# A two-layer decoder step: factors of q and k moved into v and the norm's epsilon, three more jobs ahead of the retention, third sums in banks of their own

## The chip, the cores and the metric

The kernel runs on one core of one Trainium2 chip. The metric is the device time of one execution in microseconds. The core's engines are TensorE (PE in the profile, its weight loads PEld), VectorE (DVE), ScalarE (ACT), GpSimd (POOL) and SyncE (SP), which here issues most of the transfers. Each runs its instructions in the order in which they were written out when the program was built, and waits on semaphores for the others.

## The reference, cut to what matters

The model is one inference step for 512 prompt tokens and 32 sample tokens (8 sequences of 4), 544 columns in all. Layer 0 is a gated short convolution, layer 1 a multi-scale retention with 4 heads of 256 key and 512 value channels; a SwiGLU feed-forward stage follows each. The change concerns layer 1:

```python
z = x @ w_in                                   # x is rms-normalized
q, k, v, g = split(z)                          # 4 heads each
q = rotary(q, pos)
k = rotary(k, pos) * (HEAD_DK ** -0.5)
o, S = retention_chunkwise(q, k, v, s0)        # powers of gamma(h) by position
mu, var = mean(o), mean((o - mu) ** 2)         # over the 512 value channels
of = (o - mu) * rsqrt(var + GN_EPS) * gn_g
out = (silu(g) * of) @ w_out
```

Per token there are scalar factors on q, k and v: the reciprocal root mean square of the token (the norm's gain goes elsewhere) and a power of gamma that carries the decay. A factor that belongs to the query's token scales the whole row of `o` and so leaves the group norm unchanged but for the epsilon. A factor that belongs to the key's token can as well be put on the value of that token.

## The kernel before, in words

All products are in 32-bit, split into a high and a low part, with three matmuls for each (high by high, high by low, low by high). Activations lie as channel tiles of 128 partitions by 544 tokens; the tokens are worked on in two halves of 272 columns. A *plain projection* of one 128-channel output block is 8 channel tiles x 3 x 2 halves = 48 matmuls (`project`, line 175). A *job* (`Job`, `run`, `weights7`; matmuls at line 480) makes two output blocks at once with seven products of smaller blocks in the place of eight: 7 x 4 x 3 = 84 matmuls. It adds and subtracts weight blocks on VectorE (lines 438 to 441), splits the combinations (lines 190, 191, 423 to 425), holds a first sum, a second sum and a third sum in banks, and copies or adds the sums into an SBUF tile as they come (lines 540, 543, 844). The banks are of two kinds: `sm`, four single banks in rotation (`bank`), and `mm`, two pairs of banks (`psum`).

The stages, in order of time: the convolution; feed-forward stage 0 as jobs; a stretch *ahead* of the retention, inside feed-forward stage 0's pools; the retention; feed-forward stage 1; the last norm.

The stretch ahead makes q and k of head 0 by plain projections and stores them in memory unscaled (`qk_made`, line 806), makes R, the factors by token (line 263), and then runs five jobs for gates: two blocks of head 0 and all four blocks of heads 1 and 2. Finished gates are stored in memory (`gate_made`, line 851) and fetched again in their head.

In the retention each head does, in program order: `value` (v of the head, 96 wide matmuls at lines 999 to 1001; in the midst of it the splits of q and k, the sample scores at line 1194 with line 1198, the keys' transposes, and in heads 1 and 2 the split of the head before, `held_parts`), two `state` steps, `scores`, and four `inner` products for the four blocks of 128 tokens. Between them stand *fills*, pieces of independent work for TensorE: in head 0 two gate projections and the two k projections of head 1, in heads 1 and 2 the output projections of the head before (*held products*, eight of 24 matmuls), in head 3 its own four gate projections. Four state tiles per head are loaded (line 1210), used (line 1222), updated on VectorE (line 1243) and stored (line 1244). Each block's result is normalized (lines 1144 to 1148, a power on POOL at line 227), transposed (line 1172) and multiplied into the gates (lines 1178, 1182). q and k of the next head are projected in the tail of a head: from head 1 on k twice among the last steps and q twice after all of them. From each bank the projection is multiplied with a factor table (line 959, `gt`, loaded at line 915 and scaled by R at line 942), and after the second block both are rotated with six operations (lines 969 to 974). Head 3 ends with held products of head 2 and its own output projection.

The order on each engine is made by a scheduler when the program is built; program order is its priority, and `issue_after` keeps instructions behind a named one. Buffers are rotated by tag: a new tile waits for the last user of the oldest buffer of its tag. Two lines that the change turns on:

```python
w3, w1 = [wts.tile([P, 2 * n], F32, tag="w", name=nm("w")) for _ in range(2)]
self.c = bank()[:, :HT]
```

Of the kernel before, what the change touches and what calls it, by code (L numbers as in the profile page):

```python
# [49 lines left out]
def hybrid_decode_kernel(ctx: ExitStack, tc: tile.TileContext, a: dict, o: dict):  # L50
# [52 lines left out]
    nc.vector.memset(expo, -0.5)  # L103
# [26 lines left out]
    last_load = [None]  # L130
# [93 lines left out]
    def rsqrt(out, var, n):  # L224

        nc.vector.tensor_scalar_add(out, var, EPS)
        nc.gpsimd.tensor_tensor(out, out, expo[: out.shape[0], :n], op=ALU.pow)
# [199 lines left out]

    def weights7(src1, src2, sw, adding=False):
# [6 lines left out]
        last_load[0] = nc.sync.dma_start(w1, src1)  # L435
# [25 lines left out]
    class Job:  # L461
# [3 lines left out]
        def __init__(self, srcs, operand, sw, take):  # L465
            self.srcs, self.operand, self.sw, self.take = srcs, operand, sw, take
# [27 lines left out]
        def middle(self):  # L494
            for which in self.order:
# [3 lines left out]
                elif which == 5:  # L499
                    self.c = bank()[:, :HT]  # L500
# [48 lines left out]
    def ffn(layer, next_gain, then=None):  # L549
        with ExitStack() as c1:  # L550
# [4 lines left out]
            lp = c1.enter_context(tc.tile_pool(name=f"ffl{layer}", bufs=1, reuse_waits="tile"))  # L555

# [226 lines left out]
    gate_made = {h: dram.tile([P, 4, T], F32, tag=f"g{h}", name=nm("gm")) for h in (0, *AHEAD)}  # L783

    def ahead(tp, fp, sw, operand_tiles):

# [16 lines left out]
        for which, two in ((1, pts), (0, qs)):  # L803
            for dt, pt in enumerate(two):
                each(lambda p, d: nc.scalar.activation(d, p, AF.Copy), pt, halves(made[which][:, dt, :]))
            nc.scalar.dma_start(qk_made[which], made[which])

# [25 lines left out]
        def gates(h, n):  # L833
# [19 lines left out]
            return Job([a["rtg"][h, n + i] for i in range(2)], operand, sw, summed(tile2, gate))  # L853
# [8 lines left out]
    with ExitStack() as c2:  # L862
# [47 lines left out]
        def qk_start(h):  # L910

            st = {}
            gt = kp.tile([P, 2, T], F32, tag="gt", name=nm("gt"), bufs=1)
            with tc.issue_after(last_load[0].ins) if h == 0 else ExitStack():
                nc.sync.dma_start(gt, a["gtab"][h])
            st["gt"] = gt
            st["rot"] = [
                pool.tile([P, 2, T], F32, tag=f"rot{w}", name=nm("rot"), bufs=1) for w, pool in enumerate((tp, kp))
            ]
            return st  # L920

        def qk_loaded(st):

            for t, src in ((st["rot"][1], qk_made[1]), (st["rot"][0], qk_made[0])):
                with tc.issue_after(last_load[0].ins):
                    nc.sync.dma_start(t, src)
            for which in (1, 0):
                qk_scale(st, which)
                r = st["rot"][which]
                nc.vector.tensor_mul(r, r, st["gt"][:, which, :].unsqueeze(1).to_broadcast([P, 2, T]))  # L930
# [8 lines left out]

        def qk_scale(st, which):  # L940
            gi = halves(st["gt"][:, which, :])
            nc.vector.tensor_mul(gi, gi, R)

        def qk_project(h, st, which, dt, inside=None):
# [9 lines left out]
            qk_rotate(st, which, dt, pt)  # L954

        def qk_rotate(st, which, dt, pt):
            r = st["rot"][which]
            each(
                lambda p, ri, gi: nc.vector.tensor_mul(ri, p, gi), pt, halves(r[:, dt, :]), halves(st["gt"][:, which, :])
            )  # L960
            if dt:
                rotate(r, *products())
# [4 lines left out]
        def rotate(r, t0, t1, c=slice(0, T)):  # L967
# [4 lines left out]
            nc.vector.tensor_mul(r[:, 1, :], r[:, 1, :], cos[:, c])  # L972
            nc.vector.tensor_sub(r[:, 0, :], r[:, 0, :], t0)
# [9 lines left out]
        def swapped(second, shape, dtype, name):  # L983

            return (tp if second else vp).tile(shape, dtype, tag="gate" if second else "vyl", name=nm(name), bufs=1)

        def value(h, st):
# [4 lines left out]
            for c in range(4):  # L992
# [19 lines left out]
                if c == 1:  # L1012
                    qk_split(h, st, 1)
                    qk_split(h, st, 0)
                    sample_scores(h, st)
                    for dt in range(2):
                        qsrc = st["rot"][0][:, dt, SEQ:].rearrange("p (g r s) -> p g r s", g=4, r=2)
                        for r in range(2):
                            nc.vector.tensor_scalar_mul(
                                qm[:, dt, :, r, 4 * r : 4 * r + 4], qsrc[:, :, r, :], _gamma(h) ** 4  # L1020
# [481 lines left out]
```

## Time and profile before

| what | value |
|---|---|
| median of 3 runs | 1458.92 us (1457.52 to 1459.11) |
| the profiled execution's own time | 1461.27 us |
| its span | 1459.5 us |
| mean granted TensorE clock | 0.996 |
| TensorE / VectorE / ScalarE / GpSimd busy | 99% / 68% / 45% / 10% |
| moved by the DMA engines | 201.89 MB, 138 GB/s mean |

The profile is one execution. Its page gives busy times by engine, the chain of work that ended last (followed back from the last instruction, at each step to what released it), and groups of instructions by line, engine and tile. A wait is given as "engine line <- what it waited for: total us, times, longest". A row of the timeline is start, length, engine, line, operation, out<-in, shapes, count, with the idle time before it in brackets. A row of stretches gives the busy time of each engine with the number of its instructions, then the granted clock, the share of the DMA engines and GB/s. Times within the trace are from the start of the span. TensorE's matmuls overlap, so one lasts about 290 ns although a new one starts every 125.

### The profile page before, as it was taken

How to read it: one execution, taken by the hardware profiler on the slowest of the kernel's cores; microseconds unless marked ns; L12 is line 12 of the kernel's file. 1: busy time of each engine (PE TensorE's matmuls, PEld its weight loads, DVE VectorE, ACT ScalarE, POOL GpSimd, SP SyncE). 2: the span in 40 equal slices, each digit the busy share in tenths (PEclk: the TensorE clock that was granted, in tenths of full speed). 3: DMA queues.
4: the chain of work that ended last, by engine and by line, in shares of the span. 5: the costliest groups of instructions: out<-in, count | busy, mean ns of one | idle time of the engine just before them, and what ended most of it. 6: DMA issues, size and time to landing. Idle time of an engine off the chain costs nothing.

```text
span 1459.5 us, 26302 instructions
## 1 busy us (share of the span) xinstructions
PE 1443.8 (99%) x10860; PEld 1369.0 (94%) x10860; DVE 985.7 (68%) x1536; ACT 664.0 (45%) x971; POOL 147.9 (10%) x184
## 2 busy tenths in 40 slices
PE   9999999999999999999999999999999999999997
PEld 8999999999999999997878888878999999999997
DVE  5644679847748648677575765845699848749554
ACT  5222466626526437664223032134386626537334
POOL 0100011101101003210010000000111101101002
PEclk9999999999999999999999999999999999999998
DMA  6222246636536434767353734724666635546432
GB/s 219 82 88 92 86 114 140 150 116 126 143 106 139 124 80 133 195 167 262 125 191 116 258 106 144 274 92 143 175 138 149 153 108 131 131 109 148 119 81 77
DMA packets 84297, 201.89 MB, mean 138 GB/s; under 512 B 8129, under 2 KB 25409, under 8 KB 83921
## 3 DMA queue, kind: packets, MB, share of 16 engines
q1 hardware_dynamic: 67296, 165.91, 35.9%
q0 software_dynamic: 15008, 29.18, 12.2%
q10 hardware_dynamic: 1872, 5.12, 0.9%
q8 instruction: 85, 1.39, 0.4%
q14 instruction: 36, 0.29, 0.1%
HBM read 175.11 MB, written 25.08 MB: 137 GB/s over the span
## 4 chain that ended last, share of the span: by engine, by line
PE 89%; DVE 5%; DMA 3%; ACT 1%; issue 1%; POOL 0%; SPq 0%; DVEq 0%; ACTq 0%; POOLq 0%
PE sm L480 35%; PE mm L175 33%; PE sm L175 7%; PE sm L999 2%; PE sm L1000 2%; PE sm L1001 2%; PE sm L163 2%; PE sm L164 1%; PE sm L165 1%; PE sm L1222 1%; DMA w<-in_ffgu_dram 1%; DVE wl L191 1%; DMA w<-in_rtg_dram 1%; DVE S L1243 1%; DVE ol L191 1%
## 5 line engine op out<-in xcount | busy, mean ns | idle before, releaser
L190 ACT ACTIVATE wh<-w 128x1024 fp32r<-128x1024 f32 (+4 forms) x126 | 115.8, 923 | 318.8 <-PE mm L175 204.9
L480 PE MATMUL sm<-oh,wh 128*128 128x272 f32 x744 | 215.5, 290 | 0.1
L480 PE MATMUL sm<-ol,wh 128*128 128x272 f32 x744 | 214.3, 288 | 0.7 <-DVE ol L191 0.7
L480 PE MATMUL sm<-oh,wl 128*128 128x272 f32 x744 | 213.9, 287 | 0.0
L175 PE MATMUL mm<-xh,wh 128*128 128x272 f32 x844 | 176.3, 290 | 1.1 <-ACT wh L190 1.0
L175 PE MATMUL mm<-xh,wl 128*128 128x272 f32 x844 | 174.5, 289 | 0.4 <-DMA wl<-in_rtqk_dram 0.4
L175 PE MATMUL mm<-xl,wh 128*128 128x272 f32 x844 | 173.9, 287 | 0.0
L480 PE MATMUL sm<-oh,h 128*128 128x272 f32 x568 | 164.1, 289 | 0.5 <-DVE gate L543 0.4
L480 PE MATMUL sm<-oh,l 128*128 128x272 f32 x568 | 163.5, 288 | 0.0
L480 PE MATMUL sm<-ol,h 128*128 128x272 f32 x568 | 163.5, 288 | 0.0
L273 DVE TENSOR_TENSOR x<-x,mm 128x544 f32<-128x544 f32 x90 | 64.7, 719 | 144.7 <-PE mm L175 144.7
L191 DVE TENSOR_TENSOR wl<-w,wh 128x1024 fp32r<-128x1024 f32 (+4 forms) x126 | 134.2, 1071 | 23.7 <-ACT wh L190 22.3
L480 PEld LDWEIGHTS sm<-oh,wh 128*128 128x128 f32 x744 | 139.8, 188 | 2.1 <-ACT gate L540 0.9
L423 ACT ACTIVATE wh<-w 128x1024 fp32r<-128x1024 f32 x97 | 102.8, 1060 | 83.2 <-PE sm L480 56.1
L480 PEld LDWEIGHTS sm<-ol,wh 128*128 128x128 f32 x744 | 139.8, 188 | 0.9 <-DVE ol L191 0.9
L480 PEld LDWEIGHTS sm<-oh,wl 128*128 128x128 f32 x744 | 140.3, 189 | 0.0
L426 POOL DMA_DIRECT2D wl<-in_ffgu_dram x87 | 75.6, 869 | 635.2 <-ACT wl L425 261.5
L175 PEld LDWEIGHTS mm<-xh,wh 128*128 128x128 f32 x844 | 132.2, 188 | 5.4 <-ACT wh L190 1.4
L175 PEld LDWEIGHTS mm<-xh,wl 128*128 128x128 f32 x844 | 131.6, 188 | 0.9 <-DMA wl<-in_rtqk_dram 0.6
L175 PEld LDWEIGHTS mm<-xl,wh 128*128 128x128 f32 x844 | 132.1, 188 | 0.1
L191 DVE TENSOR_TENSOR l<-w,h 128x1024 fp32r<-128x1024 f32 x98 | 93.4, 955 | 27.0 <-ACT h L190 26.4
L480 PEld LDWEIGHTS sm<-oh,h 128*128 128x128 f32 x568 | 107.2, 189 | 1.0 <-ACT wh L423 0.6
(296 smaller groups left out, 3211.8 us busy)
## 6 DMA issues: line engine op xcount, KB each, us to landing
w<-in_ffgu_dram SPq DMA_DIRECT2D x88, 512.0 KB, 3.9
wl<-in_ffgu_dram POOLq DMA_DIRECT2D x87, 256.0 KB, 4.8
w<-in_ffdn_dram SPq DMA_DIRECT2D x96, 192.0 KB, 2.5
S<-in_rets_dram SPq DMA_DIRECT2D x16, 1024.0 KB, 7.0
out_rets_dram<-S SPq DMA_DIRECT2D x16, 1024.0 KB, 4.8
w<-in_cvin_dram SPq DMA_DIRECT2D x21, 512.0 KB, 3.4
w<-in_rtqk_dram SPq DMA_DIRECT2D x16, 512.0 KB, 3.6
w<-in_rtg_dram SPq DMA_DIRECT2D x16, 512.0 KB, 4.1
```

The source lines that it names most:

```text
L163: nc.tensor.matmul(out, lh, rh, start=start, stop=False, skip_group_check=True)
L164: nc.tensor.matmul(out, lh, rl, start=False, stop=False, skip_group_check=True)
L175: last_product[0] = nc.tensor.matmul(half(pt, hf)[:, :HT], w[:, c], act[k][:, hf * HT : (hf + 1) * HT], start=(first and k == ks[0] and i ...
L190: h = nc.scalar.activation(dh, src, AF.Copy)
L191: last_low[0] = nc.vector.tensor_sub(dl, src, dh.bitcast(F32))
L273: last_residual[0] = nc.vector.tensor_add(xk, xk, p)
L423: nc.scalar.activation(wh, w, AF.Copy)
L426: nc.gpsimd.dma_start(wl[:, n:], src[:, n:], accum_op=ALU.add)
L480: last = nc.tensor.matmul(out, w[:, c], b, start=(first and k == 0 and i == 0), stop=(k == KP - 1 and i == 2), skip_group_check=True,)
L999: nc.tensor.matmul(out, xh[kt][:, ts_], wh[:, cw], start=(kt == 0), stop=False)
L1000: nc.tensor.matmul(out, xh[kt][:, ts_], wl[:, cw], start=False, stop=False)
L1001: last = nc.tensor.matmul(out, xl[kt][:, ts_], wh[:, cw], start=False, stop=(kt == KT - 1))
```

## The change

Factors. q and k are no longer multiplied with a table by token. Two small tables are made once, during the jobs ahead (`factors`): `fv`, by which v is scaled (the power of gamma times the token's norm factor squared, one norm factor being that of k), and `fe`, the epsilon of the group norm for each prompt token, divided by the square of the factor left out of q. They come from eight small loads of the table, two transposes, two powers and a few small operations. For the 32 sample tokens the factor of q is put into the masked queries and the sample scores (`gs`, from a small load `fq`).

Rotation. Since nothing is to be multiplied first, q and k go from the bank directly into products with cosine and sine: two products per block, then one sum and one difference.

Jobs ahead. Eight in the place of five: (head, first block) = (0, 0), (1, 0), (1, 2), k of 2, (2, 0), (2, 2), k of 3, (3, 0). k of heads 2 and 3 is stored unrotated (`k_made`), fetched in the head before, and rotated there behind the second state update. Heads 1 and 2 then project only q of the next head; head 3 projects only its gates 2 and 3, has no third fill, and does held products 2 and 3 in its fourth.

Banks. In the jobs ahead the third sum takes an `mm` bank.

Weights. In every job the first source is loaded before the second; the fourth combination has a pool of its own with two buffers. The stored k of head 0 is loaded behind the first weight load of the last job, q behind the second.

```diff
-    def rsqrt(out, var, n):
+    def rsqrt(out, var, n, eps=None):
-        nc.vector.tensor_scalar_add(out, var, EPS)
+        if eps is None:
+            nc.vector.tensor_scalar_add(out, var, EPS)
+        else:
+            nc.vector.tensor_add(out, var, eps)
...
     def weights7(src1, src2, sw, adding=False):
-        w3, w1 = [wts.tile([P, 2 * n], F32, tag="w", name=nm("w")) for _ in range(2)]
+        w1, w3 = [wts.tile([P, 2 * n], F32, tag="w", name=nm("w")) for _ in range(2)]
-        w4 = sw.tile([P, n], F32, tag="w4", name=nm("w4"))
+        w4 = fourth[0].tile([P, n], F32, tag="w4", name=nm("w4"))
+        second_load[0] = nc.sync.dma_start(w1, src1)
         last_load[0] = nc.sync.dma_start(w3, src2)
-        last_load[0] = nc.sync.dma_start(w1, src1)
...
-                    self.c = bank()[:, :HT]
+                    self.c = self.third()[:, :HT]
...
+        ft = tp.tile([P, 3, P], F32, tag="gu", name=nm("ft"))
+        for t in range(4):
+            nc.sync.dma_start(ft[t * NH : (t + 1) * NH, 0, :], a["gtab"][:, 0, 1, t * P : (t + 1) * P])
+        for t in range(4):
+            nc.sync.dma_start(ft[:NH, 1, t * NS : (t + 1) * NS], a["gtab"][:, 0, 1, SEQ:])
+        def factors():
+            pt = bank()
+            nc.tensor.transpose(pt[:, : 4 * NH], ft[: 4 * NH, 0, :], ident[: 4 * NH, : 4 * NH])
+            nc.tensor.transpose(pt[:, 4 * NH : 5 * NH], ft[:NH, 1, :], ident[:NH, :NH])
+            tab = pt[:, : 4 * NH].rearrange("p (t h) -> p t h", h=NH)
+            ri = ft[:, 2, :4]
+            nc.gpsimd.tensor_tensor(ri, rN[:, :4], expo[:, 6:7].to_broadcast([P, 4]), op=ALU.pow)
+            scale, back = [r.unsqueeze(2).to_broadcast([P, 4, NH]) for r in (rN[:, :4], ri)]
+            nc.vector.tensor_mul(fv[:, :4, :], tab, scale)
...
+            nc.vector.tensor_mul(fe, tab, back)
+            nc.vector.scalar_tensor_tensor(fe, fe, 256.0 * EPS, fe, op0=ALU.mult, op1=ALU.mult)
+            nc.vector.tensor_mul(fv[:, :4, :], fv[:, :4, :], scale)
...
-        jobs = [gates(0, 0)] + [gates(h, n) for h in AHEAD for n in (0, 2)]
+        jobs = [gates(*hn) for hn in ((0, 0), (1, 0), (1, 2), (2, None), (2, 0), (2, 2), (3, None), (3, 0))]
         jobs[0].prepare()
-        run(jobs, (2, 5, 6), lambda i: None, iter(()))
+        run(jobs, (2, 5, 6), lambda i: factors() if i == 1 else None, iter(()))
...
             r = st["rot"][which]
-            each(lambda p, ri, gi: nc.vector.tensor_mul(ri, p, gi), pt, halves(r[:, dt, :]), halves(st["gt"][:, which, :]))
+            if dt == 0:
+                st["rt"] = products()
+            for d, by in ((st["rt"][1 - dt], sin), (r[:, dt, :], cos)):
+                each(lambda p, d, f: nc.vector.tensor_mul(d, p, f), pt, halves(d), halves(by))
             if dt:
-                rotate(r, *products())
+                turned(r, *st["rt"])
...
             nc.vector.tensor_mul(ss, pt[:NS, 0, :NS], mask_s[:NS])
+            nc.vector.tensor_mul(ss, ss, st["gs"][:NS])
...
                 if h in AHEAD:
                     for i in range(2):
                         held_project(h, (0, 4, 2, 6)[n] + i)
-                elif h:
-                    gate_project(h, st, n)
                 elif n < 2:
                     gate_project(h, st, n + 2)
-                else:
+                elif more:
                     qk_project(h + 1, nxt, 1, n - 2)
+                elif n == 3:
+                    held_parts(h, older)
+                    held_project(h, 2)
+                    held_project(h, 3)
...
             if h in AHEAD:
                 st["gate"] = [swapped(h == 2, [P, 4, T], F32, "gate")]
                 nc.sync.dma_start(st["gate"][0], gate_made[h])
+                if more:
+                    nxt = qk_places(h + 1)
+                    nc.sync.dma_start(nxt["rot"][1], k_made[h + 1])
...
             states_update(h, st, 1)
+            if more and h:
+                with tc.issue_after(last_update[0].ins):
+                    rotate(nxt["rot"][1], *products())
...
-                    qk_project(h + 1, nxt, int(h > 0), 0)
+                    qk_project(h + 1, nxt, 0, 0)
...
             gated_pair(h, st, (yns, 4), (yn3, 3))
-            if more and h:
-                qk_project(h + 1, nxt, 0, 0)
-                qk_project(h + 1, nxt, 0, 1)
```

More of the change, by code (lines that the diff above doesn't have):

```diff
@@ L461, in hybrid_decode_kernel, with __init__ @@
     class Job:
-        def __init__(self, srcs, operand, sw, take):
-            self.srcs, self.operand, self.sw, self.take = srcs, operand, sw, take
+        def __init__(self, srcs, operand, sw, take, third=None):
+            self.srcs, self.operand, self.sw, self.take, self.third = srcs, operand, sw, take, third or bank
         order = (6, 5, 2)
@@ L555, in ffn @@
             lp = c1.enter_context(tc.tile_pool(name=f"ffl{layer}", bufs=1, reuse_waits="tile"))
+            fourth[0] = c1.enter_context(tc.tile_pool(name=f"ffw{layer}", bufs=2, reuse_waits="tile"))
             def operand_tiles(i, blocks):
@@ L1102, in gate_project @@
         def gate_project(h, st, n):
-            st.setdefault("gate", [])
-            if h == NH - 1 and n % 2 == 0:
-                pool, tag = ((kp, "gt"), (qp, "qkhl1"))[n // 2]
-                t = pool.tile([P, 2, T], F32, tag=tag, name=nm("gate"), bufs=1)
-                st["gate"].append(t)
-            elif not st["gate"]:
-                st["gate"].append(swapped(True, [P, 4, T], F32, "gate"))
+            if n == 2:
+                last = h == NH - 1
+                t = kp.tile([P, 2, T], F32, tag="gt", name=nm("gate"), bufs=1) if last else swapped(True, [P, 4, T], F32, "gate")
+                st["gate"] = [None, t] if last else [t]
             wh, wl = load_piece(a["rtg"][h, n], KT * P)
```

110 lines of the change are left out of this document (57 added, 53 removed).

## The prediction, made before the result was known

> **What bounds the kernel now.** I read the page first, then the chain that ended last, TensorE's waits, and the stages that the change touches.
>
> ```profile
> span 1459.5 us, 26302 instructions
> PE 1443.8 (99%) x10860; PEld 1369.0 (94%) x10860; DVE 985.7 (68%) x1536; ACT 664.0 (45%) x971; POOL 147.9 (10%) x184
> ```
>
> TensorE is busy for 99% of the span, so the time is the price of its matmuls plus a few stalls. The chain gives the price of each kind of matmul (start, length, what):
>
> ```profile
> 427.63 63.12 PE sm L480 x504
> 634.88 18.09 PE sm L480 x128
> 756.93 0.99 PE mm L1007 x8
> 804.08 6.23 PE mm L175 x48
> 859.67 0.99 PE mm L1007 x8
> 885.67 6.01 PE mm L175 x48
> 1265.60 36.00 PE mm L175 x288
> ```
>
> The 504 matmuls of line 480 (six seven-product jobs) take 125.2 ns each and the 288 of line 175 (plain projections) 125.0 ns. A job of 84 matmuls does two weight blocks in 63.12/6 = 10.52 us; two plain projections of 48 take 2 x 6.01 = 12.02 us. TensorE's waits and the timeline show the one large stall, between two jobs ahead of the retention:
>
> ```profile
> PE sm L480 <- DVE gate L543: 2.2, 2, 1.8
> PE sm L480 <- DVE ol L191: 0.7, 1, 0.7
> ...
> PEld sm L480 <- DVE gate L543: 2.0, 1, 2.0
> ...
> 631.24 1.36 DVE L942 TENSOR_TENSOR gt<-gt,R 128x544 f32<-128x544 f32 x2 [0.29 <-DMA gt<-in_gtab_dram]
> 633.19 1.29 DVE L930 TENSOR_TENSOR rot<-rot,gt 128x1088 f32<-128x1088 f32 x1 [0.59 <-DMA rot<-qkm]
> 634.40 0.43 DVE L543 TENSOR_TENSOR gate<-gate,sm 128x272 f32<-128x272 f32 x1
> 634.88 0.39 PE L480 MATMUL sm<-xh,h 128*128 128x272 f32 x1 [1.80 <-DVE gate L543]
> ```
>
> VectorE stands in line behind the factor table and the stored k (two transfers that it waits for), so the addition of line 543 that empties a bank comes late, and the next job's product finds no free bank: all four `sm` banks rotate through first, second and third sums alike. The stall costs more than its own length:
>
> ```profile
> 628.00:632.50 4.50, 4.50 (x35) 4.15 (x34) 3.03 (x5) 1.72 (x5) 0.87 (x1) 1.00 1.02 341
> 636.20:639.20 3.00, 3.00 (x15) 3.00 (x15) 2.75 (x6) 1.15 (x2) 0.00 (x0) 0.50 0.71 102
> 640.00:644.00 4.00, 4.00 (x34) 4.00 (x33) 3.70 (x8) 3.42 (x6) 0.53 (x1) 1.00 0.51 145
> ```
>
> In these stretches (TensorE's busy time and matmuls first, its granted clock third from the right) the clock is 1.00, then 0.50, then 1.00: 15 matmuls in 3.0 us (5.0 per us) against 34 in 4.0 us (8.5 per us). On 128 matmuls from 634.88 the chain spent 18.09 us, where 128 x 125.2 ns are 16.0; some 0.7 us of that is the usual change between products, so I take 1.4 us for the slow clock.
>
> **The change part by part.**
>
> *Work on TensorE.* Heads 2 and 3 lose two plain k projections each, head 3 two gate projections: 6 x 48 = 288 matmuls, 36.0 us by the last row of the chain. Three jobs come ahead: 3 x 84 = 252 matmuls, 63.12/2 = 31.6 us. Net -4.4 us. This holds wherever they stand, because TensorE is the bound in both stages.
>
> *Banks.* The third sums get `mm` banks; the four `sm` banks serve first and second sums, so a bank is asked for again a full job (10.5 us) after its last use. The factor table is no longer loaded or scaled on VectorE, and the stored k is fetched after the first weight load of the last job, not after the second. Both causes of the stall go: -2.0 us (the weight load's wait; the matmul's is 1.8), and -1.4 us of slow clock. What is late next there is the store-and-rotate work of VectorE, covered by the 10 us for which the weights are prepared ahead. Ends: 0 (another wait takes its place) and -3.8.
>
> *Weights in the jobs.* The order of the two loads and a second buffer for the fourth combination let one weight tile go sooner. TensorE waits for none of it in 44 jobs of the feed-forward stages, so 0.
>
> *Factors.* Two transposes of 0.1 us and a bank for some microseconds; six VectorE operations on 20 columns or fewer (0.16 us by the like row below) and two powers on POOL. Eight small loads go through SP ahead of weight loads; each holds SP 0.33 us:
>
> ```profile
> 571.53 0.33 SPq L435 DMA_DIRECT2D w<-in_rtg_dram  x1
> 581.47 0.33 SPq L905 DMA_DIRECT2D sqacc<-in_rope_dram  x1
> ...
> 582.77 0.16 DVE L226 TENSOR_SCALAR rN<-sm 128x6 f32<-128x6 f32 x1
> 583.02 2.26 POOL L227 TENSOR_TENSOR rN<-rN,expo 128x6 f32<-128x6 f32 x1 [7.36 <-DVE rN L226]
> ```
>
> SP is idle for 9.6 us between those two loads, more than 8 x 0.33 = 2.6 us. The factor operation of VectorE that needs the power waits behind POOL, 2.3 us like the row at 583.02, once, with a job of cover: +0.3 us in all, ends +0.2 and +2.5.
>
> *Sample scores.* One more multiplication on a chain that TensorE waits on a little, and a new one for the sample factors before it (early, covered by the value projection):
>
> ```profile
> 758.08 0.18 DVE L1198 TENSOR_TENSOR ss<-mm,cb 32x32 f32<-32x32 f32 x1 [2.92 <-PE mm L1194]
> ...
> PEld mm L899 <- ACT s L190: 1.5, 4, 0.4
> ```
>
> Four heads x 0.18 us at most; the weight load's wait of 0.4 is exposed in part only: +0.4 us, ends 0 and +0.7. The small load of sample factors is issued once, before the state loads, at least 6 us before use: 0. The new epsilon costs the same addition as the old: 0.
>
> *Rotation straight from the banks.* For q (and head 1's k) VectorE does four products and two sums where it did two and six: 1.4 us less per head, minus a bank held 0.7 us longer. VectorE is not the bound there: 0.
>
> *Tail of heads 1 and 2.* They lose the two projections (12 us) that stood between the last normalization and the next value projection. The tail of head 0 already has that form, with gates in the place of held products:
>
> ```profile
> 711.00:757.00 46.00, 45.99 (x296) 35.57 (x299) 38.45 (x61) 7.37 (x7) 5.22 (x5) 1.00 0.56 195
> 800.00:848.00 48.00, 47.92 (x342) 39.31 (x341) 37.49 (x56) 6.36 (x6) 3.60 (x5) 1.00 0.72 243
> 1000.00:1047.50 47.50, 47.50 (x341) 39.01 (x340) 35.03 (x61) 13.66 (x19) 4.85 (x6) 1.00 0.52 171
> ```
>
> There VectorE is busy 38.45 of 46 us and TensorE never stops: 0. What is new is k, fetched from memory and rotated on VectorE behind the second state update; this is the first rival below.
>
> *Tail of head 3.* Its gates leave, so the held products 2 and 3 (6 us) move up into the fills and nothing is left at the end but products 4, 5, 0 and 1. From the end of the scores at 1000 to the last product at 1047.5 TensorE will need 12 us less, 35.5; VectorE keeps the 35.0 us of the last row less two gate products (1.4) and one weight split (1.2), 32.4 us, or 91%. After the last inner product VectorE still has this to do:
>
> ```profile
> 1029.91 0.81 DVE L1148 TENSOR_SCALAR yn<-sm,mv,rs 128x512 f32<-128x512 f32 x1 [0.72 <-POOL rs L227]
> 1030.64 2.34 DVE L1243 SCALAR_TENSOR_TENSOR S<-S,mm 128x1024 f32<-128x1024 f32 x2
> ...
> 1034.39 2.34 DVE L1243 SCALAR_TENSOR_TENSOR S<-S,mm 128x1024 f32<-128x1024 f32 x2
> ...
> 1039.21 0.81 DVE L1148 TENSOR_SCALAR yn<-sm,mv,rs 128x512 f32<-128x512 f32 x1
> ...
> 1042.45 0.75 DVE L1178 TENSOR_TENSOR gate<-gate,mm 128x256 f32<-128x256 f32 x2 [0.77 <-PE mm L1172]
> 1043.60 2.63 DVE L191 TENSOR_TENSOR yl<-gate,yh 128x544 fp32r<-128x544 f32 x4 [0.40 <-ACT yh L190]
> ```
>
> From 1029.91 to the end of the first of the four splits (1044.3) it took 14.4 us. Less the residual additions of products 2 and 3 (0.8 and 0.7) that is 12.9 us. TensorE reaches the output projection 1047.5 - 1029.5 - 6 = 12.0 us after the last inner product, so it would wait 0.9 us, and somewhat more for what VectorE brings along as backlog at 91%. I take +1.5 us; ends 0 (the splits overtake the state updates) and +5 (a backlog of 4 us).
>
> At this length the clock matters. In this trace a stall of 2.0 us (line 543 above) brought 3.4 us at half clock. The Trainium skill, page "TensorE: Matmul & The Clock Gate", section "Part 1: The HAM clock gate", says that the half rate follows at least one idle window of about 3.4 us. By that rule a stall of 2 us in head 3 costs 2 us; by the row at 636.20 it costs 3.4. The trace decides: my 1.5 us are below the length that it showed to be punished, the upper end of 5 includes it.
>
> **The sum.** -4.4 - 3.4 + 0.3 + 0.4 + 1.5 = -5.6 us. The profiled execution took 1461.3 us, 2.4 above the median of 1458.9 shown; the same difference from the median gives 1453.3 us.
>
> **The rivals.**
>
> *k comes late in heads 1 and 2: slower.* The load of k can be issued only when the held products have left its tile, at 810.3 in head 1 (the 48 matmuls from 804.08), behind a state load and the gates:
>
> ```profile
> 808.83 0.33 SPq L915 DMA_DIRECT2D gt<-in_gtab_dram  x1
> 809.88 0.38 SPq L1210 DMA_DIRECT2D S<-in_rets_dram  x1
> 810.37 0.44 SPq L1337 DMA_DIRECT2D gate<-gm  x1
> ...
> S<-in_rets_dram SPq DMA_DIRECT2D x4, 1024.0 KB, 7.0
> gate<-gm SPq DMA_DIRECT2D x1, 1088.0 KB, 9.2
> ...
> 814.73 1.19 DVE L1243 SCALAR_TENSOR_TENSOR S<-S,mm 128x1024 f32<-128x1024 f32 x1
> ```
>
> The gates landed 9.2 us after issue, at 819.6; k takes the table's bytes but queues last, so it lands at about 820. The rotation's place on VectorE is behind the update that ends at 815.9. Engines run in a written order: if the rotation stands directly there, VectorE waits 4 us, as it waited for the stored k at 633.19, and normalizations, bank releases and the next updates wait with it. About 0.5 us is made up by the shorter q work: 3.5 us of stall plus 1.4 of slow clock, twice, +9.8: 1463.1 us. It decides for slower from 4.3 us a head (5.6 + 2.9 over two); at 2 us a head the result is about 1457. Against it: before the change VectorE waits 3.1 us for a q projection at 819.5, room into which the rotation may have been placed. Chance 0.22.
>
> *Head 3's tail starves.* 5 us in place of 1.5, with the slow clock in it: 1456.8 us, within 0.2%. For it: 91% load on VectorE; against it: its products need not all stand before the split. Chance 0.10.
>
> *The job stall stays.* The rotation of head 0 still stands amid the last job and waits for its load; the banks do not help if gate additions queue behind it and the first sum's bank is among them: 1453.3 + 3.4 = 1456.7. Chance 0.10.
>
> **How the numbers follow.** The forecast has 0.58; its own range is 1451 (no stall in head 3) to 1456. About 0.2% (2.9 us) is what a measurement of this kernel can tell from no change, so faster means below 1456.0. Faster: nearly all of the forecast and a part of each rival, 0.66; within 0.2%: the milder rivals, 0.14; slower: mostly late k, and two rivals together, 0.20. The range reaches down to 1450 (all additions hidden, load order helping 1 us) and up to the late k, 1463.
>
> **What would show it.** Right: line 480's job matmuls rise by 252 and plain 272-column ones fall by 288; no wait on line 543 and no clock of 0.50 before the retention; head 1 near 91 us long in the place of the 102.7 between its two marks of line 1007 (756.93 and 859.67); a gap of 1 to 2 us before the last output projection of head 3. Wrong: VectorE waiting on the stored k in heads 1 and 2 with TensorE waiting on state updates after it; clock rows of 0.50 inside the heads.

## The result

The changed kernel takes 1469.4 us in the median (1467.7 to 1470.9, 4 runs) against 1458.9 before: 1.0074 times as long, 95% interval 1.0056 to 1.0091. It is slower by 10.5 us. The forecast was 1453.3 with a range of 1450 to 1463, so the result lies 6 us outside the range, and on the other side of zero. The profiled execution took 1470.9 us, 1.5 above the median.

### The profile page after: what moved, and what is told of

Read it like the earlier page. It is cut to its first block, busy times and chain, and to the rows that moved or that the text cites. A ratio compares the mean times of both kernels' runs of the same rounds, so it can differ in the third digit from the quotient of the medians.

```text
span 1469.2 us, 26343 instructions
## 1 busy us (share of the span) xinstructions
PE 1449.8 (99%) x10826; PEld 1372.4 (93%) x10826; DVE 984.7 (67%) x1556; ACT 675.9 (46%) x994; POOL 150.5 (10%) x191
## 3 DMA queue, kind: packets, MB, share of 16 engines
q0 software_dynamic: 15872, 30.75, 12.7%
## 4 chain that ended last, share of the span: by engine, by line
PE 91%; DVE 3%; DMA 2%; issue 1%; ACT 1%; POOL 1%; SPq 0%; DVEq 0%; POOLq 0%; ACTq 0%
PE sm L492 35%; PE mm L181 32%; PE sm L181 7%; PE sm L1037 2%; PE sm L1039 2%; PE sm L1038 2%; PE mm L492 1%; PE sm L169 1%; PE sm L170 1%; PE sm L171 1%; PE sm L1263 1%; DMA wl<-in_rtqk_dram 1%; DMA rot<-km 1%; PE mm L1045 1%; PE mm L1281 0%
## 5 line engine op out<-in xcount | busy, mean ns | idle before, releaser
L492 PE MATMUL sm<-oh,wh 128*128 128x272 f32 x768 | 225.1, 293 | 3.6 <-ACT u L552 2.3
L492 PE MATMUL sm<-oh,wl 128*128 128x272 f32 x768 | 223.5, 291 | 1.3 <-DVE wl L433 1.3
L492 PE MATMUL sm<-ol,wh 128*128 128x272 f32 x768 | 223.8, 291 | 0.0
L181 PE MATMUL mm<-xh,wh 128*128 128x272 f32 x756 | 157.3, 289 | 0.3 <-ACT wh L196 0.2
L181 PE MATMUL mm<-xl,wh 128*128 128x272 f32 x756 | 156.7, 288 | 0.2 <-DVE xl L211 0.2
L181 PE MATMUL mm<-xh,wl 128*128 128x272 f32 x756 | 156.5, 288 | 0.4 <-DMA wl<-in_rtqk_dram 0.4
L492 PEld LDWEIGHTS sm<-oh,wl 128*128 128x128 f32 x768 | 147.3, 192 | 1.5 <-DVE wl L433 1.5
L181 PEld LDWEIGHTS mm<-xh,wh 128*128 128x128 f32 x756 | 118.9, 188 | 4.3 <-ACT wh L196 1.5
L181 PEld LDWEIGHTS mm<-xh,wl 128*128 128x128 f32 x756 | 118.4, 188 | 0.9 <-DMA wl<-in_rtqk_dram 0.6
L181 PEld LDWEIGHTS mm<-xl,wh 128*128 128x128 f32 x756 | 118.4, 188 | 0.4 <-DVE xl L211 0.4
```

What stands on the lines that cost most here:

```text
L181: last_product[0] = nc.tensor.matmul(half(pt, hf)[:, :HT], w[:, c], act[k][:, hf * HT : (hf + 1) * HT], start=(first and k == ks[0] and i ...
L492: last = nc.tensor.matmul(out, w[:, c], b, start=(first and k == 0 and i == 0), stop=(k == KP - 1 and i == 2), skip_group_check=True,)
```

## The profile after

First the head of the page of the changed kernel: its span and each engine's busy time.

```profile
span 1469.2 us, 26343 instructions
PE 1449.8 (99%) x10826; PEld 1372.4 (93%) x10826; DVE 984.7 (67%) x1556; ACT 675.9 (46%) x994; POOL 150.5 (10%) x191
```

TensorE executes 10826 matmuls where it had 10860: 288 fewer plain ones, 252 more in jobs, two transposes, which is -34. There is less work, and still TensorE is busy for 6.0 us longer and idle for 3.7 us more. The chain that ended last, in order of time, gives the stages (start, length, what); line 1045 is the former line 1007, and the two rows are the starts of heads 1 and 2:

```profile
793.27 1.00 PE mm L1045 x8
...
884.52 0.99 PE mm L1045 x8
```

Head 1 takes 884.52 - 793.27 = 91.25 us, where the forecast said "near 91" (102.74 before). The lengths of the stages by such starts, for all kernels that the argument needs (us; "before again" is a second profile of the kernel before, "old weights" the changed kernel with the old handling of the jobs' weights, both below):

| stage | before | before again | after | old weights |
|---|---|---|---|---|
| start to the first job ahead | 597.9 | 596.2 | 603.4 | 597.7 |
| ahead, to head 0 | 69.4 | 67.9 | 98.3 | 97.8 |
| head 0 | 89.6 | 89.5 | 91.5 | 93.0 |
| head 1 | 102.7 | 102.7 | 91.3 | 90.8 |
| head 2 | 102.7 | 102.7 | 90.0 | 90.0 |
| head 3, to the first job of feed-forward 1 | 115.1 | 115.1 | 104.7 | 105.3 |
| feed-forward 1 and the last norm | 382.1 | 382.1 | 390.0 | 382.8 |
| span | 1459.5 | 1456.1 | 1469.2 | 1457.3 |

Heads 1 to 3 give back about what was expected. The loss is in the two feed-forward stages, +5.5 (+7.2 against the second profile) and +7.9 us, which compute exactly what they did before. Their only edit is `weights7`: which of the two loads goes first, and a pool of its own with two buffers for the fourth combination. TensorE's waits there are new (line, what released it; total, count, longest):

```profile
PE sm L492 <- ACT u L552: 2.3, 2, 1.2
PE sm L492 <- ACT g L552: 1.5, 2, 1.3
PE sm L492 <- DVE wl L433: 1.3, 1, 1.3
```

Four of these are stalls of 1.2 to 1.3 us, near 209, 491, 1086 and 1270 us. The timeline of ScalarE around the first:

```profile
209.38 1.06 ACT L196 ACTIVATE h<-w 128x1024 fp32r<-128x1024 f32 x1 [0.80 <-PE sm L492]
210.35 0.38 ACT L552 ACTIVATE g<-sm 128x272 f32<-128x272 f32 x1
```

Line 552 copies a finished sum out of its bank, and TensorE's next product adds onto that bank, so it may not begin before the copy. Ahead of the copy in ScalarE's order stands the split of the *next* job's weights (line 196, `h<-w`), and that one has to wait until TensorE has read the old `h` for the last time. So ScalarE idles 0.80 us for TensorE, splits for 0.97, and only then makes the copy that TensorE has been waiting for.

With the old weights (the last column of the table) the split stands ahead of the copy too:

```profile
209.19 1.06 ACT L196 ACTIVATE h<-w 128x1024 fp32r<-128x1024 f32 x1 [1.07 <-PE sm L492]
210.16 1.05 ACT L432 ACTIVATE wh<-w 128x1024 fp32r<-128x1024 f32 x1
211.10 0.38 ACT L552 ACTIVATE g<-sm 128x272 f32<-128x272 f32 x1
```

but nobody waits. TensorE's own timelines, first of the changed kernel, then of old weights, tell why:

```profile
209.18 0.29 PE L492 MATMUL sm<-oh,l 128*128 128x272 f32 x1
210.78 0.39 PE L492 MATMUL sm<-oh,wh 128*128 128x272 f32 x1 [1.31 <-ACT g L552]
```

```profile
208.99 0.29 PE L492 MATMUL sm<-oh,l 128*128 128x272 f32 x1
...
209.50 0.29 PE L492 MATMUL sm<-oh,wh 128*128 128x272 f32 x1
...
210.88 0.28 PE L492 MATMUL sm<-oh,wl 128*128 128x272 f32 x1
...
211.53 0.40 PE L492 MATMUL sm<-oh,wh 128*128 128x272 f32 x1
```

After the last product with `h` and `l` there are still 15 matmuls with `wh` and `wl` to do there, 209.12 to 210.88, and they cover split and copy. A product has 12 matmuls, so they can be told apart: three end the job's product 2, and the twelve from 209.50 on are the first product of the next job, whose sum `u` ScalarE copies at 211.90. In the changed kernel two of these twelve stand ahead of the wait, at 208.00 and 208.70; the other ten follow from 213.78 on, and `u` is copied at 216.85. The matmul at 213.78 is the first of them that needs the low part of that product's weights, and VectorE makes this part (line 433) 6 us later than with the old weights. The changed kernel, then old weights:

```profile
202.52 0.69 DVE L452 TENSOR_TENSOR w<-w,w 128x512 f32<-128x512 f32 x1 [0.73 <-PE mm L181]
...
210.06 0.68 DVE L452 TENSOR_TENSOR w<-w,w 128x512 f32<-128x512 f32 x1
210.66 0.68 DVE L433 TENSOR_TENSOR wl<-w,wh 128x512 fp32r<-128x512 f32 x1
```

```profile
187.38 0.69 DVE L452 TENSOR_TENSOR w<-w,w 128x512 f32<-128x512 f32 x1
...
204.64 0.69 DVE L433 TENSOR_TENSOR wl<-w,wh 128x512 fp32r<-128x512 f32 x1
```

Line 452 makes the fourth combination, and the first row of each is that of the first job. In the new pool it is made 15 us later than in the old place, after a wait for the last products of the stage before (`PE mm L181`), and the weight tile that it reads is held until then. The second load of the next job goes out at 198.34 in place of 193.11, its combinations are made from 204.40 to 210.74 in place of 191.16 to 200.21, and the low part stands behind them. So the edit made these weights later, not sooner. That the pool lies where the stage before still reads is argued from the wait, not shown.

At 491 ScalarE waits for a load in the place of TensorE, again with the copy behind it:

```profile
489.97 0.85 ACT L196 ACTIVATE f<-w 128x768 fp32r<-128x768 f32 x1 [1.85 <-DMA w<-in_ffdn_dram]
...
492.33 0.38 ACT L552 ACTIVATE u<-sm 128x272 f32<-128x272 f32 x1
```

The stall at 1086 is VectorE's: it sums the activations' squares and makes a weight combination (line 452) ahead of the low part (line 433) that TensorE needs now:

```profile
1086.09 0.72 DVE L224 TENSOR_TENSOR sqacc<-sqacc,sqlast 128x544 f32<-128x544 f32 x1
1086.72 0.69 DVE L452 TENSOR_TENSOR w<-w,w 128x512 f32<-128x512 f32 x1
1087.32 0.69 DVE L433 TENSOR_TENSOR wl<-w,wh 128x512 fp32r<-128x512 f32 x1
...
1088.07 0.39 PE L492 MATMUL sm<-oh,wl 128*128 128x272 f32 x1 [1.32 <-DVE wl L433]
```

Here the order of the loads is at work. The combinations begin with a sum of two blocks of the second source (line 449), so with the first source loaded first none of them can be made before the second load lands. For the first job of feed-forward 1 that load is issued at 1055.36; with the old weights the sum is made before the second load is issued at all, at 1052.23 (changed kernel, then old weights):

```profile
1060.08 0.69 DVE L449 TENSOR_TENSOR w<-w 128x512 f32<-128x512 f32 x1 [1.09 <-DMA w<-in_ffgu_dram]
```

```profile
1049.51 0.69 DVE L449 TENSOR_TENSOR w<-w 128x512 f32<-128x512 f32 x1 [2.59 <-DMA w<-in_ffgu_dram]
```

Two of the four stalls are followed by slow clock. The windows of the changed kernel (TensorE's busy time and matmuls first, granted clock third from the right):

```profile
209.00:213.00 4.00, 2.69 (x18) 2.47 (x19) 4.00 (x7) 2.92 (x4) 0.37 (x1) 0.94 0.35 77
213.00:220.00 7.00, 7.00 (x35) 7.00 (x35) 3.61 (x8) 1.45 (x3) 1.69 (x2) 0.55 0.61 166
...
1084.00:1091.00 7.00, 5.56 (x34) 4.74 (x33) 6.19 (x10) 4.24 (x7) 0.87 (x1) 0.91 0.46 116
1091.00:1098.00 7.00, 7.00 (x38) 7.00 (x38) 3.00 (x6) 1.87 (x4) 1.20 (x1) 0.60 0.38 106
```

The first takes 4.00 x 0.06 + 7.00 x 0.45 = 3.4 us, the second 7.00 x 0.09 + 7.00 x 0.40 = 3.4. The four stalls (5.0 us) and the slow clock (6.8) are 11.8 us. Between the spans of after and old weights lie 11.9, but old weights has other waits: all of TensorE's waits are 8.7 us in the changed kernel and 4.7 in old weights, so waits and slow clock explain 4.0 + 6.8 = 10.8 us, and 1.1 is not followed.

## The experiments

**1. Old weights.** The changed kernel with `weights7` as before.

```diff
-w1, w3 = [wts.tile(...)]         +w3, w1 = [wts.tile(...)]
-w4 = fourth[0].tile([P, n], ...) +w4 = sw.tile([P, n], ...)
-second_load[0] = dma(w1, src1); last_load[0] = dma(w3, src2)
+second_load[0] = dma(w3, src2); last_load[0] = dma(w1, src1)
```

> The changed kernel with the weight preparation of the jobs (load order, pool of the fourth combination) as it was before. Theory: the new preparation alone makes the loss; its four stalls in the feed-forward stages (1.3 to 1.5 us each, two of them followed by 6.8 us at half clock) go, the two feed-forward stages get back the 5.2 and some 8 us that they lost, and the time is 1455 to 1458 us, below the kernel before. Rival: the stalls come from the layout and from the order that the whole change made; then they stay and the time is 1466 to 1471 us.

Measured: 1459.1 us, 1.0004 of before (0.9994 to 1.0013). The edit that I had costed at nothing costs 1469.4 - 1459.1 = 10.3 us, and all the rest of the change together is worth nothing that is clear of the noise. TensorE's waits of this kernel:

```profile
PE mm L181 <- DMA wl<-in_rtout_dram: 1.2, 1, 1.2
...
PE sm L1037 <- DVE wl L197: 0.8, 1, 0.8
```

None of the larger ones is on ScalarE's copies of line 552 or on the additions (line 555, formerly 543).

**2 and 3. One half of it each.** Experiment 2 takes back the order of the loads and keeps the new pool with its second buffer; experiment 3 takes back the pool and keeps the order.

> The changed kernel with only the old load order, the fourth combination still in two buffers of a pool of its own. Theory A (the order of the loads does it): like the kernel with all of the old preparation, 1455 to 1458 us. Theory B (the second buffer does it): like the changed kernel, 1467 to 1471 us. Both a part: in between.

> The changed kernel with only the old single buffer of the fourth combination, the loads still first source first. Theory A (order): like the changed kernel, 1467 to 1471 us. Theory B (second buffer): 1455 to 1458 us.

Measured: old order 1461.4 (1.0020, 1.0008 to 1.0032); old buffer 1464.1 (1.0043, 1.0027 to 1.0058). Against old weights the pool alone costs 2.3 us, the order alone 5.0, both together 10.3. The profiles tell which half brings which stall, first the pool alone, then the order alone:

```profile
PE sm L492 <- ACT g L552: 1.3, 1, 1.3
```

```profile
PE sm L492 <- DVE wl L433: 1.3, 1, 1.3
```

With the pool alone the stall near 209 us is there (at 211.45) and one of 1.2 us on a copy of `u` at 1261.74, but none on line 433; the first job's fourth combination waits for the stage before, until 203.20. With the order alone it is the other way round: a stall on the low part at 1082.94, none on the copies, and the fourth combination is made at 187.04. The pool's place and its second buffer were not taken apart.

**4. That edit alone, put into the kernel before.**

```diff
-last_load[0] = dma(w3, src2); last_load[0] = dma(w1, src1)
+last_load[0] = dma(w1, src1); last_load[0] = dma(w3, src2)
-w4 = sw.tile([P, n], ...)        +w4 = fourth[0].tile([P, n], ...)   # two buffers
```

> The kernel before with the new weight preparation alone. Theory: it has the same four stalls in the feed-forward stages and loses 8 to 13 us: 1467 to 1472 us. Rival (the rest of the change makes the stalls): 1457 to 1461 us.

Measured: 1467.4 us, 1.0054 (1.0039 to 1.0068), 8.9 us over the kernel before on the same chip. The cause does not need the rest of the change. Its profile has two of the four stalls, 1.3 us each at 209.99 and 1088.43, the first with slow clock behind it; those at 491 and 1270 are not there.

**5. Prepare later.** The changed kernel; in `run`, for the first job of a stage, the next job's weights are prepared after the job's middle.

```diff
-if nxt is not None: nxt.prepare()
+if nxt is not None and i: nxt.prepare()
 job.middle()
+if nxt is not None and not i: nxt.prepare()
```

> The changed kernel; in each feed-forward stage and ahead of the retention the second job's weights are prepared behind the first job's middle products in program order, no longer before. Theory: the stalls at the starts of the feed-forward stages (1.5 us each at about 209 and 1086 us, each with 6.8 us at half clock) come from ScalarE and VectorE working at the second job's weights ahead of what the first job waits for; both go and the time is 1459 to 1463 us (1469.4 less up to 9.8). Rival: the stalls come from late loads; then they stay, 1467 to 1472 us.

Measured: 1462.6 us, 1.0024 (1.0015 to 1.0033): 6.8 us of the 10.3 come back. The profile has no slow clock after either place; the stall at 1086 shrank to 0.7 us, but the one at 209 stayed (1.0 us):

```profile
213.00:220.00 7.00, 7.00 (x59) 7.00 (x59) 4.19 (x9) 3.92 (x7) 2.84 (x3) 1.00 0.69 184
```

So it works for the most part by way of the clock: the granted clock averages 0.997 to 0.998 in each of its ten runs, against 0.993 to 0.994 in the four of the changed kernel. The edit did not change the order on ScalarE there: the split still stands ahead of the copy (209.61 and 210.57) and still waits 0.80 us for TensorE. TensorE now waits for the split itself; the matmul's own row names a combination of VectorE that ended at the same time, the row of its weight load names the split:

```profile
210.72 0.19 PEld L492 LDWEIGHTS sm<-oh,h 128*128 128x128 f32 x1 [1.24 <-ACT h L196]
```

Why no slow clock follows this stall is not shown.

**6. The banks.** Old weights, and the third sums back in the `sm` banks.

```diff
-summed(tile2, gate), lambda: psum()[:, 0, :])   +summed(tile2, gate))   # k alike
```

> The changed kernel with the old weight preparation (1459.1 us) and with the third sums back in the four single banks. Theory of the prediction: the bank stall ahead of the retention returns, once or several times in eight jobs: 1461 to 1465 us. Rival: the loads of the factor table and of k made that stall alone; without the table nothing changes: 1458 to 1460 us.

Measured: 1461.1 us, 1.0017 (1.0007 to 1.0027), 2.0 us over old weights. The waits on the additions are back, beside one of 1.4 us on the bank that the factors hold:

```profile
PE sm L492 <- DVE gate L555: 1.6, 3, 0.8
```

**7. k first.** Old weights, and in heads 1 and 2 the stored k is loaded ahead of the gates.

```diff
-dma(gate, gate_made[h]); if more: nxt = qk_places(h + 1); dma(rot, k_made[h + 1])
+if more: nxt = qk_places(h + 1); dma(rot, k_made[h + 1])
+dma(gate, gate_made[h])
```

> The changed kernel with the old weight preparation, k of the next head loaded before the gates of the own head, so that it lands some 2.5 us sooner. Rival of the prediction (k late costs time): VectorE's wait of 2.9 us in head 1 goes and heads 1 and 2 get shorter by 2 us or more in all: 1455 to 1457 us. Theory: the wait lies in room that VectorE has; heads 1 and 2 stay at 90 to 91 us, 1458 to 1460 us.

Measured: 1459.6 us, 1.0005 (0.9996 to 1.0015), as old weights. VectorE's wait for the stored k in old weights is

```profile
DVE rt L1000 <- DMA rot<-km: 3.6, 2, 2.9
```

and in this kernel it is gone, while heads 1 and 2 keep their length (90.6 and 90.4 us here, 90.8 and 90.0 there). VectorE does wait at the place that the rival named, 2.9 us in head 1 and 0.7 in head 2 where the rival had 4 in each, and TensorE does not wait for it.

**8. Two repairs.** Old weights; the state updates' products count as the last product, and the last weight piece of the output projection is split without an accumulating load.

```diff
+last_product[0] =    # before the state update's nc.tensor.matmul
-load_piece(a["rtout"][h, n // 2], 2 * 4 * P, adding=n > 0)
+load_piece(a["rtout"][h, n // 2], 2 * 4 * P, adding=0 < n < 6)
```

The reason for the first is what TensorE's timeline of head 0 shows, old weights first, then before again:

```profile
752.05 0.50 PE L1280 MATMUL mm<-vs,kns 32*128 32x512 f32 x2
752.47 1.02 PE L1262 MATMUL sm<-S,qm 128*8 128x512 f32 x2
753.43 0.50 PE L1280 MATMUL mm<-vs,kns 32*128 32x512 f32 x2
753.86 1.04 PE L1262 MATMUL sm<-S,qm 128*8 128x512 f32 x6
```

```profile
718.80 0.50 PE L1238 MATMUL mm<-vs,kns 32*128 32x512 f32 x4
719.23 1.04 PE L1222 MATMUL sm<-S,qm 128*8 128x512 f32 x8
```

> The kernel of e1_weights_old (1459.1 us, equal to before) with two edits. One: the state update's products count as the last product, so that the next sample outputs are issued after them and not amid them. Two: the last weight piece of head 3's output projection is split by VectorE in place of being completed by an accumulating load. Theory (head 0's 2.0 us more come from the sample outputs' small products lying amid the state updates' products, and head 3's missing 2 us from the wait for the accumulating load): head 0 goes from 77.1 to about 75 us, the three other heads by up to 1 us each, the stall of 1.3 us at the end of head 3 goes, with a split of 1.2 us more on VectorE under cover; in all -3 us, 1456, a little under before. Rival (the interleaving only shows where TensorE waits for VectorE anyhow): head 0 stays at 77, the wait moves to the next bank, and only the stall of the load goes: 1458. Second rival (VectorE at 91% in head 3 has no room for the split): a wait on it replaces the wait on the load, 1459 to 1460.

Measured: 1462.0 us, 1.0019 (1.0008 to 1.0029), not faster than old weights. Head 0 from its second row of line 1045's kind on goes from 77.1 to 76.4 us (75.1 before) and head 3 from 105.3 to 103.9: both repairs work, the first at a third of its price. But the first jobs of feed-forward 1 now meet the stall of the changed kernel, with the old weights. ScalarE splits at 1082.01, after 0.80 us of waiting for TensorE, and copies at 1082.97, and TensorE stands still:

```profile
1081.81 0.29 PE L492 MATMUL sm<-oh,l 128*128 128x272 f32 x1
1083.41 0.40 PE L492 MATMUL sm<-oh,wh 128*128 128x272 f32 x1 [1.30 <-ACT g L552]
```

These are the instructions of 209 us again, without a product between them. The pattern isn't bound to `weights7`: it comes where no product is left to cover the split and the copy.

**9. The changed kernel profiled again.** No edit.

> The changed kernel itself, profiled once more. Theory (the half clock after a stall of 1.5 us belongs to the stall's place): both stretches of 6.8 us at half clock, after 209 and after 1086 us, appear again and the time is 1468 to 1471. Rival (the clock answers to the same stall in some executions only, as with the stall near 632 us of the kernel before, which was followed by half clock in one profile and not in the other): one or both are missing, and the time is 3.4 us shorter for each.

Measured: 1464.5 us. The slow clock after 209 is missing, though the stall is there with the same 1.3 us of waiting; that in feed-forward 1 has come, and the stalls at 491 and 1270 have not:

```profile
213.00:220.00 7.00, 7.00 (x60) 7.00 (x60) 4.77 (x11) 3.91 (x7) 2.80 (x3) 1.00 0.75 189
...
1084.00:1091.00 7.00, 7.00 (x34) 7.00 (x34) 3.78 (x9) 0.79 (x2) 1.63 (x2) 0.52 0.65 180
```

**10. The kernel before profiled again.** No edit.

> The kernel before, profiled once more. If the stall on line 543 ahead of the retention and the half clock after it belong to every execution, both are there again and the stretch from the first job to the first mark of head 0 is 69.4 us, as in the profile shown. Rival: they belong to slow executions only (that profile ran 2.4 us above the median); then the stretch is 65 to 68 us, no clock of 0.50 stands before the last stage, and the 3.4 us that the prediction took for them were not in the median.

Measured: 1457.9 us. The stall on line 543 is the same as in the first profile (1.77 us against 1.80), without slow clock behind it (the matmul in the timeline, then the window that had 15 matmuls at 0.50 in the first profile):

```profile
633.18 0.40 PE L480 MATMUL sm<-xh,h 128*128 128x272 f32 x1 [1.77 <-DVE gate L543]
```

```profile
636.20:639.20 3.00, 3.00 (x26) 2.98 (x25) 3.00 (x4) 2.84 (x4) 0.00 (x0) 1.00 0.25 44
```

**11. Both remedies.** Experiment 8 with the edit of experiment 5.

> The kernel of e8_together with the edit of e5_prepare_later too: at the first job of each stage of jobs the next job's weights are prepared after that job's middle and not before. Theory (what e8_together gained at the end of head 3, 1.4 us, and in head 0, 0.7 us, came back as the stall of 1.5 us at 1081.8 because ScalarE's split of the next job's weights stands ahead of the copy of a finished sum): that stall goes, the rest stays, 1457 us, 2 us under e8_together. Rival (the work is late as a whole at the start of the second feed-forward network, and a job later the weights are missed instead): the stall moves one job on, 1459 to 1461; and at the starts of the other stages, where e1_weights_old lost at most 1 us, the later preparation costs something: a stall on the second job's weights near 215 or 610 us.

Measured: 1461.1 us, 1.0010 (0.9999 to 1.0021). This is not the 1457 of the theory. The stall stays (the weight load waits 1.2 us from 1078.3 on, as in experiment 5 for the split itself), and the slow clock behind it came in the profile:

```profile
1080.00:1087.00 7.00, 7.00 (x34) 7.00 (x34) 4.24 (x9) 1.73 (x3) 2.09 (x2) 0.52 0.51 122
```

Of its twelve runs the fastest took 1455.9 us and the slowest 1464.0, a wider spread than that of the kernel before beside it (1457.1 to 1462.3, 16 runs).

**12. The banks alone, in the kernel before.**

```diff
-self.c = bank()[:, :HT]                         +self.c = self.third()[:, :HT]
-Job(..., sw, summed(tile2, gate))               +Job(..., sw, summed(tile2, gate), lambda: psum()[:, 0, :])
```

> The kernel before with one part of the change alone: the third sums of the jobs ahead of the retention get banks of their own. Theory (e6_third_old: the separate banks are worth 2 us; in the kernel before they would take away the stall of 1.8 to 1.9 us on the addition of line 543 near 632 us): no stall there, everything else as before, -2 us, 1457, and no half clock after 636 us in any execution. Rival (VectorE is still held up by the factor table and the stored k there, and the first sums' banks wait for it as well): the stall moves to another wait of the same job and the time stays at 1458.9. Second rival (the separate banks are taken from the four that the plain projections use at the start of the retention, which then wait for a third sum): 1459 to 1460.

Measured: 1457.3 us, 0.9984 (0.9974 to 0.9993). This is the one kernel of the study that beats both. VectorE's additions that empty banks still queue behind the table and the stored k:

```profile
630.73 0.73 DVE L942 TENSOR_TENSOR gt<-gt,R 128x544 f32<-128x544 f32 x1 [0.63 <-DMA gt<-in_gtab_dram]
631.37 0.43 DVE L543 TENSOR_TENSOR gate<-gate,sm 128x272 f32<-128x272 f32 x1
...
632.95 0.43 DVE L543 TENSOR_TENSOR gate<-gate,mm 128x272 f32<-128x272 f32 x1
```

but the third sum now leaves an `mm` bank, and TensorE's only wait for line 543 is 0.3 us in the place of 1.8:

```profile
PE mm L480 <- DVE gate L543: 0.3, 1, 0.3
```

## Why the prediction was wrong, by its steps

- **"Weights in the jobs … TensorE waits for none of it in 44 jobs of the feed-forward stages, so 0."** This is the step that failed: 10.3 us (experiments 1 and 4). I asked whether TensorE waits for the *loads* that the edit touches, and it did not. I did not ask when the work behind the loads would be done and in what order. The premise, that one weight tile goes sooner, did not hold either: at the start of feed-forward 0 the new pool makes the first job's fourth combination 15 us later and holds the tile until then, and with the new order no combination can be made before the second load. So the next job's first product, which had covered a split and a copy on ScalarE, was not ready, and preparations on VectorE came to stand ahead of a low part that TensorE needs at once. In the range the step stood with a gain alone ("load order helping 1 us"), so the range could not hold the loss.
- **Work on TensorE, -4.4.** Right. Old weights against before again: 29.9 us more ahead (forecast 31.6 - 2.0 = 29.6), heads 1 and 2 shorter by 12.0 and 12.7, head 3 by 9.8.
- **Banks, -2.0.** Right: 2.0 (experiment 6) and 2.1 (experiment 12), in either kernel. The rival that the job stall stays is refuted.
- **The slow clock, -1.4.** Wrong as a term of the median. The profiled execution of before had it and the second one did not, with the same stall. I should have seen a hint in the 2.4 us by which the profiled execution lay above the median: I subtracted the slow clock as a gain and carried the 2.4 us over besides.
- **Factors, +0.3, and sample scores, +0.4.** No wait of TensorE names them in old weights; small as forecast.
- **Tails of heads 1 and 2, 0, and the rival of the late k.** The 0 is right. VectorE waits 2.9 and 0.7 us for k (the rival said 4 each), and taking the wait away changes nothing (experiment 7). Its slack there hides it.
- **Tail of head 3, +1.5.** The size is right (12 - 9.8 = 2.2) and the cause wrong: TensorE waits 1.2 us for an accumulating load of the output weights (0.3 in the profile of experiment 6, 2.4 in that of experiment 7), not for VectorE's splits, so the rival of a tail that starves behind VectorE (5 us) falls as well. Experiment 8 took the wait away and head 3 got 1.4 us shorter.
- **Not in the sum at all.** Head 0 without its values, +2.0 us; 0.7 of it is the sample outputs' order (experiment 8), the rest lies in the time of the state updates' and sample projection's products and isn't settled. The values of head 0, +1.5 us, of which 0.8 is a weight split that arrives late. These 3.5 us, the 1.4 of slow clock, and small rests in the feed-forward stages are why the rest of the change is worth nothing in place of 5.6 us.

What stays open: why the new pool's first tile waits for the stage before (its place in memory is the likely reason), by which of its estimates the scheduler writes the late products behind the stall, what makes the stalls at 491 and 1270 come in one profile of the changed kernel and not in the other, and which executions meet the slow clock.

## What to carry to other kernels

An edit that is meant to free an input sooner has no price of zero where a scheduler writes the order: it can make another input later, and the work that covered a wait is then missing when the wait comes. Look at when a new pool's first tile can be written, and which of two loads the first dependent work needs. List which copies and splits the bounding engine waits on next, and which of its instructions stand between; and keep a copy that frees or passes on a bank ahead of any preparation that may have to wait. Before a slow clock that is seen in one profile goes into a sum, see it in a second one.

## What the runs showed of the hardware

A stall of TensorE of only 1.0 to 2.4 us can be followed by 3.4 or 6.8 us at half clock, beginning 0.4 to 1.8 us after the stall's end, and the same stall in another execution of the same kernel is not: 209 us in the two profiles of the changed kernel (1.31 and 1.30 us of waiting, clock 0.55 against 1.00 over 213 to 220 us), line 543 in the two of the kernel before. In all fourteen profiles 7 of 22 stalls of that length were followed by it (those of the first 10 us are left out), the longest, 2.4 us in experiment 7, by 3.4 us at half clock and the shortest of the seven, 1.0 us in experiment 11, by 6.8; those of 1.2 us at 491 and 1270 us in the changed kernel were not. The Trainium skill, page "TensorE: Matmul & The Clock Gate", section "Part 1: The HAM clock gate", describes a monitor with free-running windows of about 3.4 us and says that the penalty at the start of a kernel varies between runs with its phase. The lengths here (one and two times 3.4 us) and the variation agree with that. Its table lets the half rate follow an idle window of about 3.4 us; the runs here had it after stalls of 1.0 to 2.4 us, with TensorE busy on both sides. The measurement decides: a stall of 1.5 us has to be costed as 1.5 us, plus the 1.7 or 3.4 us that such a stretch at half clock loses, in some executions.
